# Two of five parked operands kept as sums, and the low parts of the gate and branch weights on VectorE

## The chip, the cores and the metric

The kernel runs on one core of a Trainium2 chip. The metric is the device time of one execution in microseconds, median of the runs. TensorE's granted clock in the profile has two levels, 2.4 GHz (shown as 1.00) and 1.2 GHz; a number between the two is a mean over a stretch.

## The reference

One block over 1024 latent tokens of width 1024 and 256 context tokens: a token mixer with two branches (a spatial gating unit A, a two-way gated linear recurrence B) and a convolutional feed-forward part, each with modulation from a conditioning vector. Cut to what the change touches:

```python
merged = sigmoid(gate_a) * (y_a @ w_a) + sigmoid(gate_b) * (y_b @ w_b)   # gate_a, gate_b: columns of h @ w_in
...
mod = silu(c) @ ada_w + ada_b                                            # six rows of 1024: shifts, scales, gates
...
a, v = split(h2 @ w_up)
out = (gelu(dwconv_grid(a)) * v) @ w_down                                # (1024 x 2816) @ (2816 x 1024)
```

Everything is float32.

## The kernel before

**Products in three terms.** Each float32 operand is split into a high part (a cast, on ScalarE) and a low part (operand minus high part). `mm3` issues three matmuls into the same PSUM bank: high by high (L98), high part of the weight by low part of the activations (L99), low part of the weight by high part of the activations (L100). So the third needs the weight's low part, two matmuls behind the first. `split_unit` makes both parts of a weight (L79 the cast, L80 the subtraction) and has GpSimd subtract where its caller names no other engine; `load_unit` loads a 512 KB weight tile (L86) and splits it.

**Buffers.** The loaded tiles (`wraw`), the high parts (`whi`) and the low parts (`wlo`) have three buffers each (`W_RAW, W_SPL = 3, 3`). All that follows shares them. A new tile takes the buffer whose last use is over; for a split that is being stored, when its store has landed.

**The gate stage** (966 to 1348 us of the trace). For each of 8 column blocks there is a gate of A, a branch product of A, a gate of B and a branch product of B; below they are called GA0 to GA7, A0 to A7, GB0 to GB7 and B0 to B7. Each of the 32 is one 512 KB weight tile and 48 matmuls of 512 columns. TensorE takes GA0, A0, GA1, A1 and so on to GA7, A7, then GB0, GB1, B0, GB2, B1 and so on to GB7, B6, B7. `gate` calls `project` (PSUM bank `pj`), `branch` calls `load_unit` itself (bank `hg`). After each tile comes one `mod_step`: a 512 KB block of `ada_w` is loaded into the single `maw` buffer (L841), and VectorE multiplies it by a column and adds it up (L842); every eighth step matmuls with a column of ones (L847) sum the partitions. The finished branch tile is multiplied by its gate on VectorE (L889 for A, L905 and L906 for B).

**Parked operands.** The feed-forward product at the end is done with sums of quarters of the matrices, seven products for eight. For six row units u of `w_down` (the last of them half as long) the generator `parts_down` loads four quarters (L107), makes the sums t1, t3, t2, t4 (L125, VectorE), splits them and b22 (L120 on ScalarE, L121 on VectorE), and stores both parts to DRAM (L123, on SP's queue). It runs between the tiles of the gate stage: two steps after each A tile to A5, three after each B tile. Its order is that of the source with the scheduler of the framework over it; every queue is served in order.

**The down stage.** `product_d` takes a function that gives the weight operand of a unit: `split_b` loads a quarter and splits it (L1278 on ScalarE, L1279 on VectorE), `parts_b` loads the two stored parts of a parked operand (L1268). The products run in the order X (two of them, 1897 to 1961), W with t2, Y with t1 (1991 to 2021), Z with t3 (2021 to 2051), Y with b22, Z with t4.

Of the kernel before, what the change touches and what calls it, by code (L numbers as in the profile page):

```python
# [8 lines left out]
F32 = mybir.dt.float32  # L9
# [7 lines left out]
P = 128  # L17
# [3 lines left out]
KC = D // P  # L21
# [14 lines left out]
def kernel(  # L36
# [6 lines left out]
    nc = tc.nc  # L43
# [12 lines left out]
    wp, close_wp = pool("wp", "left")  # L56
    dram, close_dram = pool("dram", space=DRAM)
# [6 lines left out]

    NU = (NJ // 2 + 1) // 2
    B_NAMES = ("b22", "t1", "t2", "t3", "t4")
    w_d = {(i, u): [dram.tile([P, 1024], F32, name=f"{i}{x}_d{u}") for x in "hl"] for i in B_NAMES for u in range(NU)}
    s2_d = [dram.tile([P, 1024], F32, name=f"s2_d{u}") for u in range(NU)]

    def unit_len(u):  # L70
        return min(2, NJ // 2 - 2 * u)

    W_RAW, W_SPL = 3, 3
    last_load = [None]
# [8 lines left out]
    def load_unit(src, k0, nk, c0, ncol, lo_eng=None):  # L83

        raw = wp.tile([P, 1024], F32, tag="wraw", name="wraw", bufs=W_RAW)
        last_load[0] = nc.sync.dma_start(  # L86
            out=raw.rearrange("p (k n) -> p k n", n=ncol),
            in_=src[k0 * P:(k0 + nk) * P, c0:c0 + ncol].rearrange("(k p) n -> p k n", p=P),
        )
        hi, lo = split_unit(raw, lo_eng)  # L90
        v = lambda t: t.rearrange("p (k n) -> p k n", n=ncol)
        return v(hi), v(lo)
# [9 lines left out]
    def raw_down(u, half, c0):  # L102

        raw = wp.tile([P, 1024], F32, tag="wraw", name="wraw", bufs=W_RAW)
        nk, r0 = unit_len(u), (half * (NJ // 2) + 2 * u) * P
        raw = raw[:, 0:nk * 512]
        last_load[0] = nc.sync.dma_start(  # L107
            out=raw.rearrange("p (k n) -> p k n", n=512),
            in_=w_down[0][r0:r0 + nk * P, c0:c0 + 512].rearrange("(k p) n -> p k n", p=P))
        return raw  # L110

    def parts_down():

        for u in range(NU):
            n = unit_len(u) * 512

            def keep(i, raw):
                hi = wp.tile([P, 1024], F32R, tag="whi", name="whi", bufs=W_SPL)[:, 0:n]
                lo = wp.tile([P, 1024], F32R, tag="wlo", name="wlo", bufs=W_SPL)[:, 0:n]
                nc.scalar.copy(out=hi, in_=raw)  # L120
                nc.vector.tensor_tensor(out=lo, in0=raw, in1=hi.bitcast(F32), op=ALU.subtract)  # L121
                for t, d_ in zip((hi, lo), w_d[i, u]):
                    nc.sync.dma_start(out=d_[:, 0:n], in_=t.bitcast(F32))  # L123

            sub = lambda o, a, b: nc.vector.tensor_tensor(out=o, in0=a, in1=b, op=ALU.subtract)  # L125
            b12, b11 = raw_down(u, 0, 512), raw_down(u, 0, 0)
            sub(b11, b12, b11)
            keep("t1", b11)
            yield
            b22 = raw_down(u, 1, 512)  # L130
            keep("b22", b22)
            yield
            sub(b12, b22, b12)
            keep("t3", b12)
            yield
            sub(b22, b22, b11)
            keep("t2", b22)
            yield
            b21 = raw_down(u, 1, 0)
            sub(b21, b21, b22)  # L140
            keep("t4", b21)
            yield
# [18 lines left out]
    for d in range(2):  # L161
        nc.gpsimd.affine_select(
            out=trif, in_=ones, pattern=[[1 if d == 0 else -1, P]], base=0,
# [21 lines left out]
    rows = {}  # L185
# [72 lines left out]
    for k in range(KC):  # L258
# [9 lines left out]
        if k == 4:  # L268
            norm_pair(ctok, ins_of(last_macc))
            ctp_ps = []  # L270
            for kk in range(KC // 2):
                tp = hg()
                ctp_ps.append(tp)
                for j in range(2):
                    for i in range(2):
                        nc.tensor.transpose(out=tp[:, (2 * j + i) * P:(2 * j + i + 1) * P],
                                            in_=ctok[:, i, (2 * kk + j) * P:(2 * kk + j + 1) * P], identity=ident)
# [63 lines left out]
    for q in range(4):  # L341
# [3 lines left out]
        for k in range(KC):  # L345
            wh, wl = units[k // 4]
# [192 lines left out]
    def project(off, h, dst_fn, lo_eng=None):  # L539

        wh, wl = load_unit(WI, 0, KC, off + h * P, P, lo_eng)
        for s in range(2):
            ps = pj()
            for k in range(KC):
                mm3(ps, (wh[:, k, :], wl[:, k, :]),
                    (hxh[k][:, s * 512:(s + 1) * 512], hxl[k][:, s * 512:(s + 1) * 512]), k == 0, k == KC - 1)
            dst_fn(s, ps)
# [42 lines left out]
    for h in range(NH):  # L590
# [46 lines left out]
        for st in range(2):  # L637
# [45 lines left out]
            for j in range(2):  # L683
                sp = hg()
                spv = sp.rearrange("p (i d t) -> p i d t", i=2, d=2)
                for i in range(2):
                    n = 2 * j + i
# [89 lines left out]
    for q in range(4):  # L777
# [4 lines left out]
        for n2 in range(NT // 2):  # L782
            ps = v_early[n2] if q == 0 and n2 < len(v_early) else token_major(units, n2)
            for j in range(2):
                n = 2 * n2 + j
                gelus.append(nc.scalar.activation(out=vt[n][:, q * 256:(q + 1) * 256],
                                                  in_=ps[:, j * 256:(j + 1) * 256], func=AF.Gelu_apprx_tanh))
# [70 lines left out]
    def gate(off, m):  # L858
        sg = gp.tile([P, T], F32, tag="sg", name="sg", bufs=2)

        def out_(s, ps):
            nc.scalar.activation(out=sg[:, s * 512:(s + 1) * 512], in_=ps, func=AF.Sigmoid)

        project(off, m, out_)
        mod_step()
        return sg

    def branch(w, m, yh, yl, fn):
        wh, wl = load_unit(w, 0, KC, m * P, P)
        for s in range(2):  # L870
            ps = hg()
            for k in range(KC):
                mm3(ps, (wh[:, k, :], wl[:, k, :]),
                    (yh[k][:, s * 512:(s + 1) * 512], yl[k][:, s * 512:(s + 1) * 512]), k == 0, k == KC - 1)
            fn(s, ps)
        mod_step()
# [117 lines left out]
    for q in range(4):  # L994
        units = [load_unit(w_o[0], 4 * u, 4, q * 256, 256, nc.vector) for u in range(2)]
        cs = slice(q * 256, (q + 1) * 256)
        for n in range(NT):
            ps = pj()
            for k in range(KC):
                wh, wl = units[k // 4]  # L1000
# [60 lines left out]
    for lo_, hi_, bias in ((0, 5 * NJ, False), (5 * NJ, 9 * NJ, True)):  # L1061
        crow = cv.tile([P, T], F32, tag="hd", name="crow", bufs=2)[:, 0:P]
        n = hi_ - lo_
# [4 lines left out]
        m = n + (NJ if bias else 0)  # L1068
# [167 lines left out]
    A11, A12, A21, A22 = quarter_a(0, 0), quarter_a(1, 0), quarter_a(0, 1), quarter_a(1, 1)  # L1236
# [25 lines left out]
    def parts_b(i):  # L1262
        def f(u):
            n = unit_len(u) * 512
            pair = []
            for x, d_ in zip(("whi", "wlo"), w_d[i, u]):
                t = wp.tile([P, 1024], F32R, tag=x, name=x, bufs=W_SPL)[:, 0:n]
                last_load[0] = nc.sync.dma_start(out=t.bitcast(F32), in_=d_[:, 0:n])  # L1268
                pair.append(v2(t, u))
            return pair  # L1270
        return f

    def split_b(half, c0):
        def f(u):
            raw, n = raw_down(u, half, c0), unit_len(u) * 512
            hi = wp.tile([P, 1024], F32R, tag="whi", name="whi", bufs=W_SPL)[:, 0:n]
            lo = wp.tile([P, 1024], F32R, tag="wlo", name="wlo", bufs=W_SPL)[:, 0:n]
            nc.scalar.copy(out=hi, in_=raw)  # L1278
            nc.vector.tensor_tensor(out=lo, in0=raw, in1=f32(hi), op=ALU.subtract)  # L1279
            return v2(hi, u), v2(lo, u)  # L1280
        return f

    def product_d(acc, fa, fb, first, tail=0, done=None, post=()):


        post = list(post)

        def mm(n, a, b, u, i):
            sl = slice(n * P, (n + 1) * P)
            k = 2 * u + i  # L1290
            mm3(acc[n], (a[0][:, i, sl], a[1][:, i, sl]), (b[0][:, i, :], b[1][:, i, :]), first and k == 0,
                k == HK - 1, skip_group_check=not first)

        late = []
        for u in range(NU):
            b = fb(u)
            a = parts_a(fa(u))
            if u > 0 and post:
                with tc.issue_after(ins_of(a_hi[-1])), tc.issue_after(ins_of(a_lo[-1])):
                    for f in post.pop(0):  # L1300
                        f()
            if u >= NU - tail:
                late.append((a, b, u))
                continue
            for i in range(unit_len(u)):
                for n in range(4):
                    mm(n, a, b, u, i)
        for n in range(4):
            for a, b, u in late:
                for i in range(unit_len(u)):  # L1310
                    mm(n, a, b, u, i)
            if done is not None:
                done(n)
# [30 lines left out]
    W, X = banks("wz"), banks("xy")  # L1344
# [54 lines left out]
    def run(*fs):  # L1399
        return [[lambda f=f, n=n: f(n) for f in fs] for n in range(4)]  # L1400
# [3 lines left out]
    def rows(n):  # L1404
        def f():
            with tc.issue_after(ins_of(last_load[0])):
                for _ in range(n):
                    next(more, None)
        return [f]

    product_d(X, A11, split_b(0, 0), True, post=[rows(3)] * 5)
    for n in range(4):
        nc.scalar.copy(out=p1[:, n, :], in_=X[n])
    product_d(X, A12, split_b(1, 0), False, post=[rows(4)] * 2)
    product_d(W, S2, parts_b("t2"), True, post=run(end_11a))
    Y, Z = banks("xy"), banks("wz")
    product_d(Y, S1, parts_b("t1"), True, post=run(end_w, end_11b))
    product_d(Z, S3, parts_b("t3"), True, post=run(end_y))
    product_d(Y, S4, parts_b("b22"), False, post=run(end_22))
    product_d(Z, A22, parts_b("t4"), False, tail=3, done=end_21,  # L1420
              post=[[lambda f=f, n=n: f(n) for f, n in g] for g in ends])
# [39 lines left out]
```

## Time and profile before

| | us |
|---|---|
| median of 3 runs | 2124.27 (2121.86 to 2124.37) |
| profiled execution, its own time | 2126.31 |
| its span | 2124.6 |
| TensorE busy | 2051.6 (97%) |
| VectorE / ScalarE / GpSimd busy | 1258.5 / 783.1 / 561.8 |
| gate stage, 966 to 1348 | 382.0 |
| Y and Z of the down stage, 1991 to 2050.7 | 59.7 |

The profiled execution lies 2.0 us over the median, and 1.7 us of it lie around the span. In the rows below a time in front is microseconds from the span's start; a bracket after a row is how long the engine was idle before it and what ended that. PE is TensorE, DVE VectorE, ACT ScalarE, POOL GpSimd, SP the queue that issues most DMAs.

### The profile page before, as it was taken

How to read it: one execution, taken by the hardware profiler on the slowest of the kernel's cores; microseconds unless marked ns; L12 is line 12 of the kernel's file. 1: busy time of each engine (PE TensorE's matmuls, PEld its weight loads, DVE VectorE, ACT ScalarE, POOL GpSimd, SP SyncE). 2: the span in 40 equal slices, each digit the busy share in tenths (PEclk: the TensorE clock that was granted, in tenths of full speed). 3: DMA queues.
4: the chain of work that ended last, by engine and by line, in shares of the span. 5: the costliest groups of instructions: out<-in, count | busy, mean ns of one | idle time of the engine just before them, and what ended most of it. 6: DMA issues, size and time to landing. Idle time of an engine off the chain costs nothing. (4 is left out here: it accounts for less than half of the span.)

```text
span 2124.6 us, 27641 instructions
## 1 busy us (share of the span) xinstructions
PE 2051.6 (97%) x11138; PEld 1736.9 (82%) x11138; DVE 1258.5 (59%) x1742; ACT 783.1 (37%) x1103; POOL 561.8 (26%) x328
## 2 busy tenths in 40 slices
PE   8889999999999999999999998999999999999997
PEld 3879889889889889888777876898778888887886
DVE  4784364374375362444343445548699888896665
ACT  3765355255355341222213222324333333334222
POOL 2131212122121110221112111134476666610001
PEclk9989999999999999999999999999999999999999
DMA  7630111111111011115564766631222222266676
GB/s 268 208 90 21 50 40 40 41 41 48 41 32 60 31 56 54 41 40 179 188 227 152 236 225 224 207 96 38 67 78 81 89 90 84 75 242 223 223 272 228
DMA packets 215138, 251.04 MB, mean 118 GB/s; under 512 B 8852, under 2 KB 166873, under 8 KB 213986
## 3 DMA queue, kind: packets, MB, share of 16 engines
q1 hardware_dynamic: 212977, 244.29, 35.0%
q10 hardware_dynamic: 2032, 4.99, 0.6%
q8 instruction: 87, 1.43, 0.3%
q14 instruction: 42, 0.34, 0.1%
HBM read 193.39 MB, written 55.85 MB: 117 GB/s over the span
## 5 line engine op out<-in xcount | busy, mean ns | idle before, releaser
L80 POOL TENSOR_TENSOR wlo<-wraw,whi 128x1024 fp32r<-128x1024 f32 x88 | 220.5, 2509 | 747.8 <-ACT whi L79 697.4
L98 PE MATMUL pj<-hxh,whi 128*128 128x512 f32 x896 | 355.7, 397 | 9.0 <-ACT whi L79 8.8
L100 PE MATMUL pj<-hxh,wlo 128*128 128x512 f32 x896 | 354.3, 395 | 8.0 <-POOL wlo L80 8.0
L99 PE MATMUL pj<-hxl,whi 128*128 128x512 f32 x896 | 353.1, 394 | 1.0 <-POOL hxl L456 1.0
L79 ACT CAST whi<-wraw 128x1024 fp32r<-128x1024 f32 x124 | 129.1, 1048 | 300.1 <-PE pj L99 131.9
L1178 DVE SCALAR_TENSOR_TENSOR acc<-apad,cw,acc 128x1024 f32<-128x1024 f32 x176 | 226.3, 1286 | 20.8 <-ACT acc L1176 17.4
L98 PEld LDWEIGHTS pj<-hxh,whi 128*128 128x128 f32 x896 | 170.2, 190 | 45.8 <-ACT whi L79 11.9
L100 PEld LDWEIGHTS pj<-hxh,wlo 128*128 128x128 f32 x896 | 169.9, 190 | 44.8 <-POOL wlo L80 10.6
L99 PEld LDWEIGHTS pj<-hxl,whi 128*128 128x128 f32 x896 | 170.0, 190 | 34.8 <-POOL hxl L456 1.3
L98 PE MATMUL pj<-whi,hxh 128*128 128x256 f32 x512 | 145.3, 285 | 0.0
L99 PE MATMUL pj<-wlo,hxh 128*128 128x256 f32 x512 | 145.1, 284 | 0.0
L100 PE MATMUL pj<-whi,hxl 128*128 128x256 f32 x512 | 144.9, 283 | 0.0
L371 DVE TENSOR_TENSOR_SCAN b<-scanm,g 128x512 f32<-128x512 bf16 (+1 forms) x24 | 26.3, 1094 | 176.7 <-ACT g L618 174.7
L842 DVE SCALAR_TENSOR_TENSOR acc<-maw,sc,acc 128x1024 f32<-128x1024 f32 x32 | 51.3, 1603 | 86.3 <-DMA maw<-in_ada_w_dram 83.2
L99 PEld LDWEIGHTS pj<-wlo,hxh 128*128 128x128 f32 x512 | 98.2, 192 | 0.4 <-issue 0.2
L98 PEld LDWEIGHTS pj<-whi,hxh 128*128 128x128 f32 x512 | 98.1, 192 | 0.4 <-issue 0.2
L100 PEld LDWEIGHTS pj<-whi,hxl 128*128 128x128 f32 x512 | 98.3, 192 | 0.0
L173 POOL TENSOR_TENSOR rs<-ss,mhalf 128x4 f32<-128x4 f32 (+1 forms) x21 | 19.6, 934 | 261.6 <-DVE ss L737 210.8
L120 ACT CAST whi<-wraw 128x1024 fp32r<-128x1024 f32 (+1 forms) x30 | 29.4, 979 | 133.4 <-DVE wraw L125 22.6
L173 POOL TENSOR_TENSOR ss<-ss,mhalf 128x1 f32<-128x1 f32 x16 | 11.2, 699 | 246.9 <-DVE ss L1333 213.4
L98 PE MATMUL pj<-whi,mh 128*128 128x256 f32 x256 | 73.6, 288 | 1.3 <-ACT mh L801 1.3
L100 PE MATMUL pj<-whi,ml 128*128 128x256 f32 x256 | 73.2, 286 | 0.8 <-DVE ml L802 0.8
(471 smaller groups left out, 5156.7 us busy)
## 6 DMA issues: line engine op xcount, KB each, us to landing
wraw<-in_w_in_dram SPq DMA_DIRECT2D x96, 512.0 KB
wraw<-in_ffn_w_up_dram SPq DMA_DIRECT2D x44, 512.0 KB
maw<-in_ada_w_dram SPq DMA_DIRECT2D x32, 512.0 KB
wraw<-in_ffn_w_down_dram SPq DMA_DIRECT2D x30, 512.0 KB
hid_d<-hd SPq DMA_DIRECT2D x22, 512.0 KB
ring<-in_ada_w_dram SPq DMA_DIRECT2D x8, 1024.0 KB
ring<-in_x_dram SPq DMA_DIRECT2D x4, 1024.0 KB
yb_d<-og SPq DMA_DIRECT2D x8, 512.0 KB
```

The lines of the kernel that those rows point to most:

```text
L79: nc.scalar.copy(out=hi, in_=raw)
L80: (lo_eng or nc.gpsimd).tensor_tensor(out=lo, in0=raw, in1=hi.bitcast(F32), op=ALU.subtract)
L98: nc.tensor.matmul(ps, lhsT=ah, rhs=bh, start=first, stop=False, **kw)
L99: nc.tensor.matmul(ps, lhsT=ah, rhs=bl, start=False, stop=False, **kw)
L100: nc.tensor.matmul(ps, lhsT=al, rhs=bh, start=False, stop=last, **kw)
L120: nc.scalar.copy(out=hi, in_=raw)
L173: nc.gpsimd.tensor_tensor(out=dst, in0=src, in1=mhalf[:, :n], op=ALU.pow)
L371: nc.vector.tensor_tensor_scan(out=b, data0=scanm[:, :n], data1=g, initial=0.0, op0=ALU.mult, op1=ALU.add)
L842: nc.vector.scalar_tensor_tensor(out=acc, in0=aw, scalar=sc[:, k, 0:1], in1=acc, op0=ALU.mult, op1=ALU.add)
L1178: nc.vector.scalar_tensor_tensor(out=grid(acc), in0=src, scalar=w_, in1=grid(acc), op0=ALU.mult, op1=ALU.add)
```

## The change

t1 and t3 are no longer split in the gate stage. Their sum is stored once, straight from the raw buffer, and the down stage loads the sum and splits it there, in the way in which it splits the operands that were never parked. The other three (b22, t2, t4) stay as they are. `gate` and `branch` name VectorE for the low part of their weights.

```diff
-    w_d = {(i, u): [dram.tile([P, 1024], F32, name=f"{i}{x}_d{u}") for x in "hl"] for i in B_NAMES for u in range(NU)}
+    w_d = {(i, u): [dram.tile([P, 1024], F32, name=f"{i}{x}_d{u}") for x in ("s" if i in ("t1", "t3") else "hl")]
+           for i in B_NAMES for u in range(NU)}
...
             def keep(i, raw):
+                if len(w_d[i, u]) == 1:
+                    nc.sync.dma_start(out=w_d[i, u][0][:, 0:n], in_=raw)
+                    return
                 hi = wp.tile([P, 1024], F32R, tag="whi", name="whi", bufs=W_SPL)[:, 0:n]
...
-        project(off, m, out_)
+        project(off, m, out_, nc.vector)
...
-        wh, wl = load_unit(w, 0, KC, m * P, P)
+        wh, wl = load_unit(w, 0, KC, m * P, P, nc.vector)
...
-    def split_b(half, c0):
+    def summed_b(i):
         def f(u):
-            raw, n = raw_down(u, half, c0), unit_len(u) * 512
+            raw = wp.tile([P, 1024], F32, tag="wraw", name="wraw", bufs=W_RAW)[:, 0:unit_len(u) * 512]
+            last_load[0] = nc.sync.dma_start(out=raw, in_=w_d[i, u][0][:, 0:unit_len(u) * 512])
+            return raw
+        return split_b(f)
...
-    product_d(Y, S1, parts_b("t1"), True, post=run(end_w, end_11b))
-    product_d(Z, S3, parts_b("t3"), True, post=run(end_y))
+    product_d(Y, S1, summed_b("t1"), True, post=run(end_w, end_11b))
+    product_d(Z, S3, summed_b("t3"), True, post=run(end_y))
```

SP's queue around GA4, before (L86 loads a gate or branch weight, L107 a quarter of `w_down`, L123 stores a part, h or l, of a parked operand; the row with t1h stands ahead of GA3's weight, the one with b22l ahead of GA4's):

```order
L123 DMA t1h_d_97<-whi 128x1024
L86 DMA wraw<-in_w_in_dram 128x8x128
L123 DMA t1l_d_98<-wlo 128x1024
L86 DMA wraw<-in_w_branch_a_dram 128x8x128
L107 DMA wraw<-in_ffn_w_down_dram 128x2x512
L123 DMA b22h_d_85<-whi 128x1024
L123 DMA b22l_d_86<-wlo 128x1024
L86 DMA wraw<-in_w_in_dram 128x8x128
L123 DMA t3h_d_121<-whi 128x1024
L123 DMA t3l_d_122<-wlo 128x1024
```

and after (t3s is the sum; the line numbers are 1 to 4 higher):

```order
L87 DMA wraw<-in_w_in_dram 128x8x128
L87 DMA wraw<-in_w_branch_a_dram 128x8x128
L108 DMA wraw<-in_ffn_w_down_dram 128x2x512
L120 DMA t3s_d_114<-wraw 128x1024
L127 DMA b22h_d_85<-whi 128x1024
L127 DMA b22l_d_86<-wlo 128x1024
L87 DMA wraw<-in_w_in_dram 128x8x128
L87 DMA wraw<-in_w_branch_a_dram 128x8x128
```

One store of t3's sum, ahead of the stores of b22 and of GA4's weight, stands for the two of its parts behind it; t1's has gone ahead of this piece.

SP's queue around GB7, before (its weight is the last row):

```order
L123 DMA t4h_d_139<-whi 128x1024
L841 DMA maw<-in_ada_w_dram 128x1024
L123 DMA t4l_d_140<-wlo 128x1024
L123 DMA t1h_d_105<-whi 128x512
L107 DMA wraw<-in_ffn_w_down_dram 128x512
L841 DMA maw<-in_ada_w_dram 128x1024
L123 DMA t1l_d_106<-wlo 128x512
L123 DMA b22h_d_93<-whi 128x512
L123 DMA b22l_d_94<-wlo 128x512
L86 DMA wraw<-in_w_in_dram 128x8x128
```

and after:

```order
L127 DMA t4h_d_127<-whi 128x1024
L845 DMA maw<-in_ada_w_dram 128x1024
L127 DMA t4l_d_128<-wlo 128x1024
L120 DMA t1s_d_100<-wraw 128x512
L108 DMA wraw<-in_ffn_w_down_dram 128x512
L845 DMA maw<-in_ada_w_dram 128x1024
L127 DMA b22h_d_93<-whi 128x512
L127 DMA b22l_d_94<-wlo 128x512
L87 DMA wraw<-in_w_in_dram 128x8x128
```

The weight keeps its place behind b22's stores; one store is gone, and t1's needs no cast.

VectorE from GB6 to GB7, before (L125 sums, L121 subtracts for a parked operand):

```order
L125 TENSOR_TENSOR wraw<-wraw 128x1024
L905 TENSOR_TENSOR sg<-hg,sg 128x512
L842 SCALAR_TENSOR_TENSOR acc<-maw,sc,acc 128x1024
L906 TENSOR_TENSOR mg_8111<-mg_8111,sg 128x512
L121 TENSOR_TENSOR wlo<-wraw,whi 128x1024
L125 TENSOR_TENSOR wraw<-wraw 128x512
L842 SCALAR_TENSOR_TENSOR acc<-maw,sc,acc 128x1024
L121 TENSOR_TENSOR wlo<-wraw,whi 128x512
```

and after (L81 is the low part of a weight: GB6's, then B5's):

```order
L81 TENSOR_TENSOR wlo<-wraw,whi 128x1024
L846 SCALAR_TENSOR_TENSOR acc<-maw,sc,acc 128x1024
L81 TENSOR_TENSOR wlo<-wraw,whi 128x1024
L909 TENSOR_TENSOR sg<-hg,sg 128x512
L129 TENSOR_TENSOR wraw<-wraw 128x1024
L910 TENSOR_TENSOR mg_8099<-mg_8099,sg 128x512
L846 SCALAR_TENSOR_TENSOR acc<-maw,sc,acc 128x1024
L125 TENSOR_TENSOR wlo<-wraw,whi 128x1024
L129 TENSOR_TENSOR wraw<-wraw 128x512
```

The low parts of the weights stand between multiply-accumulates (L842, now L846), each of which waits for its own load. TensorE's order is the same before and after; GpSimd loses 32 rows.

## Rows read from the trace of the kernel before

**Rows 1.** Busy time by window: length, each engine's busy us (instructions), clock, DMA share, GB/s.
```profile
966.00:1348.00 382.00, 365.11 (x1559) 292.99 (x1557) 175.13 (x161) 96.48 (x112) 73.26 (x30) 0.98 0.62 205
```

**Rows 2.** Waits of TensorE, 966 to 1348: line, waited for: total us, times, longest.
```profile
PE pj L98 <- ACT whi L79: 8.8, 4, 5.4
PE pj L100 <- POOL wlo L80: 8.0, 5, 1.9
```

**Rows 3.** Windows around GA4, after it, around GA6 and GB7 (columns of rows 1).
```profile
1056.80:1074.70 17.90, 14.08 (x50) 10.60 (x49) 6.88 (x8) 5.08 (x6) 4.72 (x2) 0.81 0.58 184
1074.70:1085.60 10.90, 10.90 (x50) 9.01 (x48) 2.55 (x2) 2.60 (x3) 4.79 (x2) 1.00 0.86 274
1107.10:1123.20 16.10, 13.21 (x51) 10.16 (x50) 7.21 (x4) 3.08 (x4) 4.74 (x2) 0.89 0.41 134
1303.90:1324.40 20.50, 13.90 (x51) 10.50 (x50) 10.32 (x8) 3.73 (x5) 4.75 (x2) 0.83 0.48 148
```

**Rows 4.** Timeline at GA4: start, duration, engine, line, operation, idle time before it.
```profile
1051.39 0.61 SPq L123 DMA_DIRECT2D t3h_d<-whi  x1
...
1058.15 1.04 ACT L79 CAST whi<-wraw 128x1024 fp32r<-128x1024 f32 x1 [6.29 <-DMA t3h_d<-whi]
...
1059.24 0.50 PE L98 MATMUL pj<-hxh,whi 128*128 128x512 f32 x1 [1.87 <-ACT whi L79]
...
1062.00 0.79 PE L100 MATMUL pj<-hxh,wlo 128*128 128x512 f32 x1 [1.95 <-POOL wlo L80]
```

**Rows 5.** Timeline at GB7 (columns of rows 4).
```profile
1296.44 0.43 SPq L107 DMA_DIRECT2D wraw<-in_ffn_w_down_dram  x1
...
1300.87 0.62 ACT L120 CAST whi<-wraw 128x512 fp32r<-128x512 f32 x1 [4.33 <-DMA wraw<-in_ffn_w_down_dram]
...
1302.97 0.38 SPq L86 DMA_DIRECT2D wraw<-in_w_in_dram  x1
...
1308.59 1.04 ACT L79 CAST whi<-wraw 128x1024 fp32r<-128x1024 f32 x1 [6.60 <-DMA wraw<-in_w_in_dram]
...
1309.68 0.80 PE L98 MATMUL pj<-hxh,whi 128*128 128x512 f32 x1 [5.39 <-ACT whi L79]
```

**Rows 6.** Groups by line, 966 to 1348: busy us, mean ns, idle us before and releasers.
```profile
L80 POOL TENSOR_TENSOR wlo<-wraw,whi 128x1024 fp32r<-128x1024 f32 x30 | 73.3, 2442 | 305.6 <-ACT whi L79 257.4 <-DMA t3l_d<-wlo 16.9 <-DMA t2l_d<-wlo 15.9
L842 DVE SCALAR_TENSOR_TENSOR acc<-maw,sc,acc 128x1024 f32<-128x1024 f32 x32 | 51.3, 1603 | 86.3 <-DMA maw<-in_ada_w_dram 83.2 <-DMA acc<-in_ada_b_dram 3.1
...
L121 DVE TENSOR_TENSOR wlo<-wraw,whi 128x1024 fp32r<-128x1024 f32 (+1 forms) x30 | 35.9, 1195 | 29.4 <-ACT whi L120 14.6 <-DMA t3l_d<-wlo 4.2 <-DMA t2l_d<-wlo 3.5
```

**Rows 7.** Durations min/median/max in ns, waits for the load, and two timeline rows.
```profile
L842 DVE SCALAR_TENSOR_TENSOR acc<-maw,sc,acc x32: 1271/1285/3397, 977.9 to 1309.9; 128x1024 f32<-128x1024 f32 x32
...
  DMA maw<-in_ada_w_dram: 83.2, 26
...
L80 DVE TENSOR_TENSOR wlo<-wraw,whi x2: 1212/1214/1216, 1342.4 to 1344.2; 128x1024 fp32r<-128x1024 f32 x2
...
1108.79 3.38 DVE L842 SCALAR_TENSOR_TENSOR acc<-maw,sc,acc 128x1024 f32<-128x1024 f32 x1 [6.21 <-DMA maw<-in_ada_w_dram]
...
1108.74 2.35 POOL L80 TENSOR_TENSOR wlo<-wraw,whi 128x1024 fp32r<-128x1024 f32 x1 [23.80 <-ACT whi L79]
```

**Rows 8.** Down stage: windows of Y and Z; groups by line, 1913 to 2060.
```profile
1991.00:2020.80 29.80, 29.80 (x133) 24.66 (x132) 17.97 (x21) 7.96 (x12) 0.00 (x0) 1.00 0.55 192
2020.80:2050.70 29.90, 29.90 (x134) 24.75 (x133) 14.43 (x16) 5.89 (x6) 0.00 (x0) 1.00 0.75 261
...
L99 PE MATMUL xy<-wlo,b21h 128*128 128x512 f32 x79 | 31.4, 398 | 1.2 <-DVE wlo L1279 1.2
L98 PE MATMUL xy<-whi,b21h 128*128 128x512 f32 x78 | 31.2, 400 | 1.1 <-ACT whi L1278 1.1
...
L1279 DVE TENSOR_TENSOR wlo<-wraw,whi 128x1024 fp32r<-128x1024 f32 (+1 forms) x9 | 9.9, 1103 | 4.7 <-ACT whi L1278 4.6
L1278 ACT CAST whi<-wraw 128x1024 fp32r<-128x1024 f32 (+1 forms) x9 | 8.6, 953 | 5.9 <-DMA wraw<-in_ffn_w_down_dram 3.5 <-PE xy L100 2.4
```

More of the change, by code (lines that the diff above doesn't have):

```diff
@@ L1271, in parts_b, with plain_b, split_b, f @@
         return f
-    def split_b(half, c0):
+    def summed_b(i):
         def f(u):
-            raw, n = raw_down(u, half, c0), unit_len(u) * 512
+            raw = wp.tile([P, 1024], F32, tag="wraw", name="wraw", bufs=W_RAW)[:, 0:unit_len(u) * 512]
+            last_load[0] = nc.sync.dma_start(out=raw, in_=w_d[i, u][0][:, 0:unit_len(u) * 512])
+            return raw
+        return split_b(f)
+    def plain_b(half, c0):
+        return split_b(lambda u: raw_down(u, half, c0))
+    def split_b(load):
+        def f(u):
+            raw, n = load(u), unit_len(u) * 512
             hi = wp.tile([P, 1024], F32R, tag="whi", name="whi", bufs=W_SPL)[:, 0:n]
@@ L1409, in rows @@
         return [f]
-    product_d(X, A11, split_b(0, 0), True, post=[rows(3)] * 5)
+    product_d(X, A11, plain_b(0, 0), True, post=[rows(3)] * 5)
     for n in range(4):
         nc.scalar.copy(out=p1[:, n, :], in_=X[n])
-    product_d(X, A12, split_b(1, 0), False, post=[rows(4)] * 2)
+    product_d(X, A12, plain_b(1, 0), False, post=[rows(4)] * 2)
     product_d(W, S2, parts_b("t2"), True, post=run(end_11a))
     Y, Z = banks("xy"), banks("wz")
-    product_d(Y, S1, parts_b("t1"), True, post=run(end_w, end_11b))
-    product_d(Z, S3, parts_b("t3"), True, post=run(end_y))
+    product_d(Y, S1, summed_b("t1"), True, post=run(end_w, end_11b))
+    product_d(Z, S3, summed_b("t3"), True, post=run(end_y))
     product_d(Y, S4, parts_b("b22"), False, post=run(end_22))
```

## The prediction, made before the changed kernel ran

> **What bounds the kernel now.** I read the page's busy shares and the TensorE line first: TensorE is busy for nearly the whole span, so only its waits and the stretches at a lower granted clock can be saved. I then cut the trace by stage. The change touches the gate stage, 966 to 1348 us, and two products of the down stage, 1991 to 2051 us. In the gate stage [rows 1] TensorE works 32 weight tiles of 48 matmuls; a tile takes 10.9 us where nothing waits, as the last window of [rows 3] shows (1074.7 to 1085.6, clock 1.00). 32 × 10.9 = 349 us, some 5 us go to the small matmuls with the ones column, and the stage takes 382. The view of TensorE's waits names what is over [rows 2]: 8.8 us for the high part of an input-projection weight (ScalarE, line 79) and 8.0 us for the low part (GpSimd, line 80), nine waits and 16.8 us in all. The windows around the three worst [rows 3] show what such a wait costs beside itself: granted clock 0.81, 0.89 and 0.83 instead of 1.00, so 17.9 × 0.19 + 16.1 × 0.11 + 20.5 × 0.17 = 8.7 us at the 1.2 GHz level, always behind a wait. Together **25.5 us** can be had in this stage, no more. In the down stage from 1917 to 2098 the view of waits holds no TensorE row, so nothing can be had there.
>
> **Why it waits.** Two mechanisms. The first is the low part itself: the third matmul of a group wants it 0.46 us after the first, and GpSimd needs 2.44 us on average [rows 6]. At gate weight GA4 (1059.24) TensorE starts with the high part, then stops 1.95 us for the low one [rows 4]. The second is the parked splits: gate and branch weights share three high and three low buffers with the splits that are being stored. At GA4 the high buffer was held by the store of t3's high part, issued at 1051.39; the cast ended its wait for it at 1058.15, 6.8 us later [rows 4]. Near the stage's end (GB7) the weight's load is the last of a series on SP's queue: b22's at 1296.44, the weight itself only at 1302.97; cast at 1308.59, and TensorE stood 5.39 us [rows 5].
>
> **Low parts on VectorE.** 32 subtractions leave GpSimd and take 1.214 us each on VectorE, as the two that stand there now show [rows 7]. Each low part ends 2.44 − 1.21 = 1.2 us earlier behind its cast, if VectorE is free. The five low-part waits shrink from 8.0 to 8.0 − 5 × 1.2 = 2.0 us at most, with no other edit. VectorE pays 32 × 1.21 = 38.8 us; twelve parked subtractions of line 121 leave (12 × 1.195 = 14.3), and its multiply-accumulates of line 842 shorten: median 1.285, mean 1.603 [rows 6, 7]; the long ones lie beside GpSimd (1108.79, 3.38 us long, beside 1108.74, 2.35 long). With GpSimd silent, 32 × 0.32 = 10.2 us come back. Net +14 us on 175 of 382 [rows 1]: an average of half busy, so the place in the queue decides, not the sum. The price of that is the second rival.
>
> **Two operands stored as sums.** t1 and t3 leave out a cast, a subtraction and one store per unit (six units each, the last half as long), and take no high or low buffer; in exchange the raw buffer stays taken until the one store lands. At GA4 the hop "b22's store lands, cast of t3, t3's store lands" (6.8 us and more) goes, and the weight's buffer is behind b22's store instead. A multiply-by-gate of a finished branch tile (line 889) now stands behind such low parts too; the bank it frees is wanted a whole tile later, so 0. I worked the new orders of SP, VectorE and ScalarE forward by hand, with 4.5 to 5 us for a 512 KB transfer, between the 4.4 us of b22's half-sized load (1296.44 to 1300.87) and the 5.6 to 6.8 us of the weight's load at GB7 and t3's store at GA4 [rows 4, 5]. GA3 has its high part near 1024, wanted at 1031.7. Its split frees the next raw buffer that much earlier, b22 lands near 1037.5, sum 1.2, t3's store to 1043.5, GA4's load to 1048, cast 1049, low part 1050.3; it is wanted at 1055.1 (all earlier waits gone). GA5 and GA6 come out 8 to 9 us early. So in the first half everything goes: about 8.2 us of waits and 5.2 of clock, **−13.4**. In the second half GB3, GB4 and GB5 come out 5 to 8 us early. GB6 is closer: low part 0.7 us ahead of need. GB7: counted from GB6's start (1280.3), t1's load is issued about 4 us earlier than now (low part of GB6 and of the branch weight 1.2 us sooner each, and no wait at GB6), b22 no longer waits behind t1's split, and the weight's load is issued at +15 instead of +22.5; the high part is there at +20.5 to +21.6, the low at +21.8 to +22.9, wanted at +21.8. That is on the edge: a hop of the chain that takes 1 us more makes TensorE wait, and the clock may fall once (1.8 to 3.5 us, by [rows 3]). I put 3 us of waits and 1.5 of clock back, between 0 and 8: second half 12.1 − 4.5, **−7.6**.
>
> The Trainium skill (SBUF — State Buffer, section "The DMA setup-cost knee (why "@ 1 MiB" ≠ asymptote)") gives a transfer as 2 us plus its bytes over 436 GB/s, which makes an estimate of 3.2 us for 512 KB. The transfers of [rows 4, 5] took 5.6 and 6.8, so the trace does not agree here, where several are under way at once. By the page GB6 and GB7 would be early and the sum −25.5; by the rows it is −21.
>
> **The down stage.** In products Y and Z one raw load replaces two part loads; twelve casts (0.95 us) and twelve subtractions (1.10 us) come in [rows 8]. Per product that is 6 × 1.10 = 6.6 us on VectorE (busy 18.0 and 14.4 of 29.8) and 5.7 us on ScalarE (8.0 and 5.9): cover is there. The raw buffers are otherwise unused in these products, so the loads can go ahead of those they replace. The nearest row for what the split costs TensorE is the first product of this stage, which splits in the same way: 1.2 us of waits for a low part (and 1.1 for a high one) in twelve units, at its start [rows 8]. Below nothing is excluded, since TensorE does not wait in Y and Z now. I take **0**, up to +2.3 for one late start. Transfers of 5.8 MB each way go; no engine waits for their sum, so 0.
>
> **Sum.** −13.4 − 7.6 + 0 = −21.0 on the profiled run: 2126.3 − 21.0 = 2105.3; that run is 2.0 us over the median, so I forecast **2104.5** (by the bounds 2099 to 2112).
>
> **Rivals.** (a) *Transfers are fast enough at GB6 and GB7*: nothing comes back, −25.5, **2100**. The lighter DMA load speaks for it, the lengths in [rows 4, 5] against. This is what the page's rule gives. Chance 0.13. (b) *The parked part buys nothing*: the raw buffers, now held until a store lands, make the weights' loads late by what the split buffers cost now, and the high-part waits stay. Then only the low parts gain: 8.0 − 2.0 = 6, **2118 to 2120**, or **2122** if the clock falls once more. For it: store (to 6.8 us), load (5.6), cast and subtraction lie in one chain at GA4, 15 us and more. Against: 22 us (two tiles) are there. Chance 0.13. (c) *VectorE's queue takes the wait over*, and the kernel is slower. The low part now stands behind a multiply-accumulate that waits for its load: line 842 made VectorE idle 83.2 us before 26 of 32 [rows 6, 7], 3.2 us each, and takes 1.3 itself. A low part caught there comes 4.5 us late, and each such tile costs that, since GpSimd, which waited for nobody, had 2.4. From seven full catches (31 us) on the gain is gone and more; at eight it is 36 − 25.5 = +10.5, **2135**. For it: in VectorE's new order 14 of the low parts have such a row one or two places ahead. Against: apart from GB6 and GB7 the low parts have 5 us and more to spare, and the loads run ahead of them. Chance 0.12. The Trainium skill (PSUM — Partial Sum Buffer, section "Engine vs sequencer instructions") says that VectorE's queue is strictly first in, first out; the 83.2 us of idleness before line 842, with finished casts behind it, agree.
>
> **How the numbers follow.** Forecast 0.60, (a) 0.13, (b) 0.13, (c) 0.12, others 0.02. A measurement of this kernel tells 0.2% (4.2 us) from no change: faster is below 2120, slower above 2128.5. Faster: 0.60 + 0.13 + 0.03 of (b) and 0.01 = 0.77; same: 0.10 of (b) and 0.01 = 0.11; slower 0.12. The range goes from 2097 (case (a) and the run's scatter) to 2121 (most of (b)); (c) and the rest of (b) lie outside.
>
> **What would show it.** Right: the gate stage near 361 us; TensorE's waits there 1 to 5 us in all and only at GB6 and GB7; clock 1.00 around GA4 and GA6; GpSimd busy about 73 us less [rows 1, 6]; line 842 near 1.29 us; no TensorE wait in Y and Z. Wrong: high-part waits at GA3, GA4 or GA6 again, behind the landing of a sum's store (b); low-part waits whose VectorE row follows an idle line 842 (c); or a stage that does not shorten although the waits are gone.

## The result, and the profile after

The changed kernel takes **2100.47 us** (median of 4 runs, 2095.67 to 2101.46) beside 2124.32 of the kernel before: a ratio of 0.988 (95% interval 0.9856 to 0.9904), 25 us. Run again later beside other runs of before it took 2097.69 (ratio 0.9876, 0.9856 to 0.9897). The profiled execution took 2101.34, its span is 2099.6, 25.0 us less than before.

The stages, from the start and end of TensorE's matmuls in the timelines of the two profiled executions (the gate stage ends here at 1347.5 and 1326.1, where the last of the small matmuls with the ones column behind B7 starts):

| us | before | after | difference | forecast |
|---|---|---|---|---|
| start of GA0 | 966.5 | 968.4 | +1.8 | 0 |
| GA0 to GB0 (first half of the gate stage) | 191.2 | 178.2 | −13.1 | −13.4 |
| GB0 to the end of the stage (second half) | 189.8 | 179.6 | −10.2 | −7.6 |
| end of the stage to the first up projection of the feed-forward part | 157.4 | 153.4 | −4.0 | 0 |
| up projection | 391.8 | 390.5 | −1.3 | 0 |
| the two X products | 64.3 | 65.1 | +0.8 | 0 |
| W, Y, Z and Y again, each | 29.92 | 29.92 | 0 | 0 |
| last product | 33.4 | 34.4 | +1.0 | 0 |

I read the rows of +1.8, −1.3, +0.8 and +1.0 as scatter: over the ten runs below GA0 starts between 964.3 and 969.4, and the up projection takes 388.2 to 391.6, in no order of what was changed.

The view of busy time by window, the gate stage alone before and after (length, then TensorE, its weight loads, VectorE, ScalarE, GpSimd with instruction counts, clock, DMA share, GB/s):

```profile
966.50:1347.50 381.00, 364.11 (x1554) 292.49 (x1553) 174.13 (x161) 95.62 (x111) 73.26 (x30) 0.98 0.62 205
```

```profile
968.30:1326.10 357.80, 356.47 (x1554) 288.90 (x1553) 183.01 (x183) 85.90 (x99) 0.00 (x0) 1.00 0.61 200
```

GpSimd is empty, VectorE has 9 us more, the clock is 1.00. The view of TensorE's waits in the same stretch of after, which answers [rows 2]:

```profile
PE pj L99 <- ACT whi L80: 0.8, 1, 0.8
PE pj L101 <- DVE wlo L81: 0.5, 1, 0.5
```

Of 16.8 us in nine waits 1.3 in two are left, both at GB7, and in the second profile of the same kernel there is none. The timeline there (start, duration, what it waited for), beside [rows 5]:

```profile
1278.00 0.87 SPq L108 DMA_DIRECT2D wraw<-in_ffn_w_down_dram  x1
...
1284.73 0.38 SPq L87 DMA_DIRECT2D wraw<-in_w_in_dram  x1
...
1290.05 1.04 ACT L80 CAST whi<-wraw 128x1024 fp32r<-128x1024 f32 x1 [6.79 <-DMA wraw<-in_w_in_dram]
...
1291.15 0.50 PE L99 MATMUL pj<-hxh,whi 128*128 128x512 f32 x1 [0.80 <-ACT whi L80]
1291.48 0.40 PE L100 MATMUL pj<-hxl,whi 128*128 128x512 f32 x1
1292.41 0.50 PE L101 MATMUL pj<-hxh,wlo 128*128 128x512 f32 x1 [0.53 <-DVE wlo L81]
```

The weight's load is issued 5.6 us before TensorE is done with the tile in front (1291.15 − 0.80 = 1290.35); before it was 1.3 us (1309.68 − 5.39 = 1304.29, and 1302.97). The groups by line, answering [rows 6] and [rows 7]:

```profile
L846 DVE SCALAR_TENSOR_TENSOR acc<-maw,sc,acc 128x1024 f32<-128x1024 f32 x32 | 41.1, 1284 | 45.2 <-DMA maw<-in_ada_w_dram 45.1
L81 DVE TENSOR_TENSOR wlo<-wraw,whi 128x1024 fp32r<-128x1024 f32 x32 | 39.0, 1221 | 60.2 <-ACT whi L80 50.5 <-DMA t4l_d<-wlo 4.5 <-DMA b22l_d<-wlo 3.4
```

```profile
L846 DVE SCALAR_TENSOR_TENSOR acc<-maw,sc,acc x32: 1277/1284/1289, 981.8 to 1292.3; 128x1024 f32<-128x1024 f32 x32
```

The multiply-accumulates are all 1.28 us long (before: 1.271 to 3.397), and the time for which they make VectorE wait for their load fell from 83.2 to 45.1 us. The windows of Y and Z, answering [rows 8]:

```profile
1965.00:1994.80 29.80, 29.80 (x133) 24.68 (x132) 23.89 (x27) 13.18 (x18) 0.00 (x0) 1.00 0.29 97
1994.90:2024.70 29.80, 29.80 (x133) 24.66 (x133) 19.38 (x21) 9.37 (x10) 0.00 (x0) 1.00 0.43 147
```

VectorE has 5 to 6 us more in each, TensorE is without a gap as before.

### The profile page after: what moved, and what is told of

Its sections match the earlier page's. It is cut to its first block, busy times and chain, and to the rows that moved or that the text cites. A ratio compares the mean times of both kernels' runs of the same rounds, so it can differ in the third digit from the quotient of the medians.

```text
span 2099.6 us, 27515 instructions
## 1 busy us (share of the span) xinstructions
PE 2044.8 (97%) x11138; PEld 1734.7 (83%) x11138; DVE 1275.0 (61%) x1774; ACT 782.9 (37%) x1103; POOL 482.9 (23%) x296
## 5 line engine op out<-in xcount | busy, mean ns | idle before, releaser
L81 POOL TENSOR_TENSOR wlo<-wraw,whi 128x1024 fp32r<-128x1024 f32 x56 | 142.6, 2551 | 421.2 <-ACT whi L80 419.0
L81 DVE TENSOR_TENSOR wlo<-wraw,whi 128x1024 fp32r<-128x1024 f32 x68 | 82.6, 1220 | 114.5 <-ACT whi L80 104.8
L1015 POOL TENSOR_TENSOR xa<-tg,a2b 128x256 f32<-128x256 f32 x32 | 29.7, 929 | 450.2 <-DMA a2b<-mod_d 404.3
L100 PE MATMUL pj<-wlo,mh 128*128 128x256 f32 x256 | 72.4, 283 | 0.0
```

What stands on the lines that cost most here:

```text
L81: (lo_eng or nc.gpsimd).tensor_tensor(out=lo, in0=raw, in1=hi.bitcast(F32), op=ALU.subtract)
L100: nc.tensor.matmul(ps, lhsT=ah, rhs=bl, start=False, stop=False, **kw)
L1015: nc.gpsimd.tensor_mul(out=xa[n][:, cs], in0=tg, in1=a2b[:, cs])
```

## The experiments

Gains below are worked out from the ratios, as a share of 2124.3 us; their intervals are 3 to 7 us to either side.

**Each half of the change alone.** The theory on trial was that of the prediction: the parked splits hold the buffers, so the sums carry most of the gain (some 15 to 20 us), and the move to VectorE carries about 6. The rival: the engine alone.

The sums alone, low parts on GpSimd:

```diff
-        project(off, m, out_, nc.vector)
+        project(off, m, out_)
...
-        wh, wl = load_unit(w, 0, KC, m * P, P, nc.vector)
+        wh, wl = load_unit(w, 0, KC, m * P, P)
```

> t1 and t3 are stored as sums, the low parts of the gate and branch weights stay on GpSimd. My theory (the store of a parked split in front of a weight's buffer is the cause, the 2.4 us of GpSimd only makes it worse): in the changed kernel the weights up to GB5 had their parts 5 us or more ahead, so 1.2 us more each does no harm there, and the waits at GA3, GA4, GA6 stay away; every hop of the chain to GB6 and GB7 is 1.2 us longer, so 3 to 7 us of waits come there. Gate stage 361 to 368 us instead of 358, time 2104 to 2112. Rival (GpSimd's low part binds whatever comes before): about 8 us of low-part waits as before, with their clock, time 2112 to 2118. VectorE's line for the multiply-accumulate stays at a mean of 1.5 us or more by both.

Measured: 2110.11 (ratio 0.9931, 0.9914 to 0.9949). The first half of the gate stage is without a wait (178.1 us), the second has not gained at all: 191.2 us, 189.8 before. The windows and the waits:

```profile
969.40:1147.50 178.10, 178.10 (x779) 144.51 (x777) 66.51 (x59) 36.85 (x43) 39.82 (x17) 1.00 0.57 185
1147.50:1338.80 191.30, 182.89 (x777) 147.06 (x776) 99.01 (x95) 48.67 (x57) 34.14 (x14) 0.97 0.62 203
```

```profile
PE pj L99 <- ACT whi L80: 5.0, 2, 3.3
PE pj L101 <- POOL wlo L81: 3.4, 2, 1.7
```

The time lies in the theory's range and the place of the waits is right (GB6 and GB7); the waits are 8.4 us instead of 3 to 7, and the stage takes 369.4 us instead of 361 to 368.

The low parts alone, all five operands in parts (the edit is the reverse of the one above, on the kernel before):

> The low parts of the gate and branch weights go to VectorE, all five parked operands keep their two stored parts. My theory: the high-part waits stay (7 to 9 us, GA4 and GB7 above all), the low-part ones shrink from 8.0 to 1 to 3 us, and the clock falls as often: time 2115 to 2120. Rival (engines alone: 1.2 us less on each hop that frees a raw buffer and an undisturbed VectorE pull the whole chain forward): waits of 2 to 4 us in all, time 2103 to 2108. A third possibility is that the longer VectorE queue makes it 2124 or more.

Measured: **2097.03** (0.9867, 0.9847 to 0.9888). The theory had 2115 to 2120; the rival's 2103 to 2108 was still too slow. The gate stage is at its floor, 355.9 us, and the view of TensorE's waits holds no row in it:

```profile
967.50:1323.40 355.90, 355.90 (x1555) 289.00 (x1553) 196.11 (x195) 96.76 (x111) 0.00 (x0) 1.00 0.67 222
```

So the move to VectorE does everything that the whole change does, and the high-part waits go with it although every parked split is still there. The theory fell. The rival was right in kind (shorter hops pull the whole chain forward), and too small in size.

One sum at a time, low parts on VectorE: first t3, then t1 (the same edit the other way round).

```diff
-    w_d = {(i, u): [dram.tile([P, 1024], F32, name=f"{i}{x}_d{u}") for x in ("s" if i in ("t1", "t3") else "hl")]
+    w_d = {(i, u): [dram.tile([P, 1024], F32, name=f"{i}{x}_d{u}") for x in ("s" if i in ("t3",) else "hl")]
...
-    product_d(Y, S1, summed_b("t1"), True, post=run(end_w, end_11b))
+    product_d(Y, S1, parts_b("t1"), True, post=run(end_w, end_11b))
```

> As the changed kernel, but only t3 is a sum; t1 keeps its two parts. Theory: t3's split stood ahead of GA4 and GA6, t1's ahead of GA3 and GB7; so GA4 and GA6 stay clean, GB7 waits 3 to 5 us for its high part with one fall of the clock: 2104 to 2110. Rival (every parked split is alike, half of them gives half): 2110 to 2113.

> As the changed kernel, but only t1 is a sum; t3 keeps its two parts. Theory: the waits at GA4 and GA6 come back for the high part (2 to 4 us in all, one or two falls of the clock), GB7 stays within 2 us: 2105 to 2112. Rival (half gives half): 2110 to 2113.

Measured: 2097.20 (0.9874, 0.9848 to 0.9900) with t3 alone, 2096.95 (0.9868, 0.9844 to 0.9892) with t1 alone. Both expectations missed in the same way: the waits hardly came back where a part was parked again. With t3 alone GB7 waits 1.7 us instead of 3 to 5 (1.3 in the first profile of the changed kernel), with t1 alone nothing waits.

**What the engine does: its duration, or its silence.** Why should a high part come earlier because low parts are made elsewhere? The timelines show what follows a low part. Before, GA3 and A3:

```profile
1031.53 2.36 POOL L80 TENSOR_TENSOR wlo<-wraw,whi 128x1024 fp32r<-128x1024 f32 x1 [18.31 <-ACT whi L79]
1040.28 2.39 POOL L80 TENSOR_TENSOR wlo<-wraw,whi 128x1024 fp32r<-128x1024 f32 x1 [6.39 <-ACT whi L79]
```

```profile
1033.91 0.38 SPq L86 DMA_DIRECT2D wraw<-in_w_branch_a_dram  x1
1042.69 0.38 SPq L107 DMA_DIRECT2D wraw<-in_ffn_w_down_dram  x1
1047.60 0.34 SPq L123 DMA_DIRECT2D b22h_d<-whi  x1
```

GA3's low part ends at 1033.89, and A3's load is issued at 1033.91. A3's low part ends at 1042.67, and b22's load is issued at 1042.69; then come b22's split, its store, t3's split, its store ([rows 4]) and GA4. The low part is the last reader of the raw buffer, so it lies in one chain with what is loaded after it. It is so not only here: from 966.5 to 1347.5 the view of the waits of SP's queue (line, waited for: total us, times, longest) has 14 weight loads and 13 loads of quarters that waited for a low part on GpSimd, 27 of the 56 loads into raw buffers that the trace has there:

```profile
SPq L86 <- POOL wlo L80: 51.1, 14, 5.3
SPq L107 <- POOL wlo L80: 37.9, 13, 5.0
```

The same stretch with only the low parts moved:

```profile
1026.26 1.23 DVE L80 TENSOR_TENSOR wlo<-wraw,whi 128x1024 fp32r<-128x1024 f32 x1 [3.34 <-DMA t1l_d<-wlo]
...
1032.10 1.23 DVE L80 TENSOR_TENSOR wlo<-wraw,whi 128x1024 fp32r<-128x1024 f32 x1 [2.32 <-ACT whi L79]
```

```profile
1027.52 0.38 SPq L86 DMA_DIRECT2D wraw<-in_w_branch_a_dram  x1
1033.36 0.38 SPq L107 DMA_DIRECT2D wraw<-in_ffn_w_down_dram  x1
1038.19 0.34 SPq L123 DMA_DIRECT2D b22h_d<-whi  x1
```

Here, too, each load is issued 0.03 us behind the end of a low part; from one load to the next it is 5.84 us (before 8.78), and b22's store has come forward by 9.4 us. Of these 2.9 us the shorter low part is 1.2; most of the rest is A3's load, which takes 3.5 us up to its cast instead of 5.2, and why it does no run shows. The casts of A3's high part, before and with the low parts moved, and below them the cast for GA4:

```profile
1039.14 1.05 ACT L79 CAST whi<-wraw 128x1024 fp32r<-128x1024 f32 x1 [7.25 <-DMA wraw<-in_w_branch_a_dram]
```

```profile
1031.02 1.05 ACT L79 CAST whi<-wraw 128x1024 fp32r<-128x1024 f32 x1 [4.43 <-DMA wraw<-in_w_branch_a_dram]
...
1047.30 1.05 ACT L79 CAST whi<-wraw 128x1024 fp32r<-128x1024 f32 x1 [4.86 <-DMA t3h_d<-whi]
```

GA4's cast still waits for the store of t3's high part, as in [rows 4]; but TensorE comes to GA4 only at 1056.58, 9 us later. Three experiments tell apart what in that counts. The first does the subtraction twice on VectorE:

```diff
         (lo_eng or nc.gpsimd).tensor_tensor(out=lo, in0=raw, in1=hi.bitcast(F32), op=ALU.subtract)
+        if twice:
+            lo_eng.tensor_tensor(out=lo, in0=raw, in1=hi.bitcast(F32), op=ALU.subtract)
...
-        project(off, m, out_, nc.vector)
+        project(off, m, out_, nc.vector, True)
...
-        wh, wl = load_unit(w, 0, KC, m * P, P, nc.vector)
+        wh, wl = load_unit(w, 0, KC, m * P, P, nc.vector, True)
```

> The kernel with only the low parts moved to VectorE (no waits in the gate stage, 2097), with each of these 32 subtractions done twice there in a row, so that a low part takes 2.44 us as it did on GpSimd; GpSimd stays silent. Theory A (duration: the low part frees the raw buffer, and so every load, sum and store behind it, and 1.2 us on each of these hops was what the chain lacked): the waits come back, 8 to 20 us in all, time 2108 to 2126. Theory B (GpSimd itself: it made VectorE's instructions longer, 10 us of them, and the order of the queues was another): the waits stay under 4 us, time 2096 to 2103.

Measured: 2116.59 (0.9957, 0.9943 to 0.9971): 9 us gained instead of 28, as theory A has it. The gate stage takes 377.8 us, 21.9 more than with one subtraction and 3.2 less than before; GpSimd is silent, the multiply-accumulates are undisturbed, and the waits are back, high-part ones first:

```profile
PE pj L100 <- ACT whi L79: 10.9, 2, 8.0
PE pj L102 <- DVE wlo L82: 5.2, 3, 2.9
```

```profile
L844 DVE SCALAR_TENSOR_TENSOR acc<-maw,sc,acc 128x1024 f32<-128x1024 f32 x32 | 41.0, 1281 | 30.4 <-DMA maw<-in_ada_w_dram 30.3
```

They lie at GA6, GB6 and GB7; GA3 and GA4 are clean. The second subtraction also keeps VectorE busy longer (229.7 of 377.8 us, 34 us more than with one); this experiment doesn't tell how much of the 21.9 us is that. Nor does it tell what the 9 us that stay gained come from: 3.2 of them lie in the stage and 4.0 behind it.

The other two move the low parts of one half of the weights, with all operands in parts: the gates', then the branches'.

```diff
-        project(off, m, out_)
+        project(off, m, out_, nc.vector)
```

> All five operands parked in parts, low parts on VectorE for the 16 gate weights alone; the 16 branch weights stay on GpSimd. Local theory (the low part matters where the third matmul waits for it, and all such waits were at gates): nearly all of the gain, 2097 to 2103. Chain theory (each low part frees a raw buffer): half of the slack is missing, 2 to 8 us of waits come back, high-part ones first, 2102 to 2112.

```diff
-        wh, wl = load_unit(w, 0, KC, m * P, P)
+        wh, wl = load_unit(w, 0, KC, m * P, P, nc.vector)
```

> The other half: low parts on VectorE for the 16 branch weights alone, gates on GpSimd. Local theory: nothing is gained, since no wait was at a branch weight, 2121 to 2127. Chain theory: a gain of 6 to 15 us although no branch weight ever waited, 2109 to 2118, with the low-part waits at the gates shorter or gone.

Measured: gates alone 2115.11 (0.9950, 0.9933 to 0.9968), branches alone **2109.94** (0.9926, 0.9906 to 0.9947). The waits, gates moved, then branches moved:

```profile
PE pj L98 <- ACT whi L79: 8.4, 5, 4.0
PE pj L100 <- DVE wlo L80: 2.1, 4, 0.5
```

```profile
PE pj L98 <- ACT whi L79: 5.7, 1, 5.7
PE pj L100 <- POOL wlo L80: 4.4, 3, 2.4
```

With the gates moved the low-part waits shrink to what the prediction said, 2.1 us, and the high-part ones stay at 8.4. The gain is 10.6 us: in the profile the stage is 7.8 us shorter (373.2 us), and behind it the 4.0 us are gone as in the changed kernel. Both expectations missed: 2115.1 is slower than either range, and 10.5 us of waits are left where the chain theory had 2 to 8. With the branches moved, where TensorE had not waited once, 15.7 us are gained, as the chain theory had it (2109 to 2118); the low-part waits at the gates, still on GpSimd, fall from 8.0 to 4.4 and the high-part ones from 8.8 to 5.7. Their loads start earlier: counted from GA0's start, GA4's is issued at 78.0 us instead of 84.3, and at 73.8 with all low parts moved. With the gates alone moved it is issued at 84.2: up to GA4 the low parts of the gates brought nothing forward by themselves. So the branch half bears the chain theory out; what a gate's low part adds to the chain was not taken apart. The two halves make 26 us together, the whole move 28; with these intervals that doesn't tell whether they simply add.

**What the sums are worth.** The changed kernel again, beside the runs of the last three:

> The changed kernel again, beside the same runs of the kernel before as the three others, for its distance to the kernel with only the low parts moved (2097.0). If the two sums cost something: 2099 to 2102, with the wait at GB7 again; if they are indifferent: 2096 to 2099.

Measured: 2097.69 (0.9876, 0.9856 to 0.9897), with no wait at GB7 this time. Beside 2097.03 without the sums they are indifferent. Then the sums carried on, first to all operands (t2 and t4 as sums too, b22 not parked; the diff shows this one), then only b22 taken out, with t2 and t4 in parts:

```diff
-    w_d = {(i, u): [dram.tile([P, 1024], F32, name=f"{i}{x}_d{u}") for x in ("s" if i in ("t1", "t3") else "hl")]
+    w_d = {(i, u): [dram.tile([P, 1024], F32, name=f"{i}{x}_d{u}") for x in ("s" if i != "b22" else "hl")]
...
-            keep("b22", b22)
...
-    product_d(W, S2, parts_b("t2"), True, post=run(end_11a))
+    product_d(W, S2, summed_b("t2"), True, post=run(end_11a))
...
-    product_d(Y, S4, parts_b("b22"), False, post=run(end_22))
-    product_d(Z, A22, parts_b("t4"), False, tail=3, done=end_21,
+    product_d(Y, S4, plain_b(1, 512), False, post=run(end_22))
+    product_d(Z, A22, summed_b("t4"), False, tail=3, done=end_21,
```

> The changed kernel taken to its end: t1, t2, t3 and t4 are all stored as sums, b22 is not parked at all (the down stage loads it from w_down), so no parked operand is split in the gate stage; every product of the down stage splits its own. Low parts on VectorE. Theory (with the low parts on VectorE the chain has slack and the sums neither help nor harm; the down stage has cover for the splits): gate stage at its floor of 356 us, Y, Z and W at 29.9, the wait of the last product for t4's part (2.4 us) smaller: 2094 to 2099. Rival (each sum holds a raw buffer until its store lands, and three per unit make the weights late): 3 to 10 us of high-part waits in the second half, 2100 to 2110.

> The changed kernel, with b22 not parked (the down stage loads it from w_down and splits it); t2 and t4 stay in parts. Two stores per unit less and no raw buffer held longer. Theory: 2095 to 2099, the same as the changed kernel within its scatter, with no wait at GB7. Rival (the split in the product after Z is not covered, since VectorE is busier there): 1 to 4 us of waits in that product, 2099 to 2103.

Measured: 2095.57 (0.9857, 0.9833 to 0.9881) and 2096.58 (0.9862, 0.9831 to 0.9893), both where the theory had them. With no split parked at all the gate stage stands at the floor that it had with all five parked, although VectorE has 162.4 us of work there instead of 196.1 and the DMA queues move 167 GB/s instead of 222:

```profile
964.30:1320.10 355.80, 355.80 (x1554) 289.00 (x1553) 162.38 (x164) 68.53 (x83) 0.00 (x0) 1.00 0.53 167
```

W, Y, Z and the second Y take 29.92 us in it as in all kernels here, with all seven products splitting their weights; the last one takes 31.9 us, and 33.3 in the kernel with the low parts alone. It is the fastest of all that ran, by 1.5 us on the kernel with the low parts alone, which the runs don't tell from nothing.

## Why the prediction was right, and where it was not

The time (2104.5 forecast, 2100.5 measured, range 2097 to 2121) and the sign were right. The reading of the gate stage was right too: 25.5 us were to be had, and the stage is 25.1 us shorter in the kernels that reach its floor. What the time came from was not, and that the total came out all the same is in part luck: both edits draw on the same 25 us, the forecast spent 21 of them, and the edit that it priced as the smaller one, the low parts, takes them all by itself. The sum also slips at its end: 2105.3 less the 2.0 us by which the profiled run lies over the median is 2103.3 and not 2104.5. And its 8.7 us "at the 1.2 GHz level" are what the lower clock cost; at a level of half the speed the time spent there is twice that.

- **The step that failed** is "The five low-part waits shrink from 8.0 to 8.0 − 5 × 1.2 = 2.0 us at most, with no other edit", and with it the price of rival (b), 2118 to 2122. It counted a low part only where TensorE waits for it. The waits it counted did shrink to 2.1 us (gates alone); but a low part is also the last reader of a raw buffer, and 27 loads of the stage waited for one. Measured: 28 us for the low parts alone instead of 6. The prediction had used this very effect in working both edits forward together (GA3's split "frees the next raw buffer that much earlier", and GB6's low part brings GB7's loads forward), and left it out where it priced the low parts alone. So the words of rival (b), that the parked part buys nothing, came true behind the low parts, and its price was 21 us off.
- **The sums** were left with −21 us less those 6. Alone they do bring 15 (2110.1), but all in the first half and after the stage's end; behind the low parts they bring nothing that can be measured (2097.7 with them, 2097.0 without). The hand-worked forward run of the changed orders was right that GA3 and GA4 would be in time and GB7 on the edge. Counted from GA0 and GB6, GA3's high part came within 1 us of it, GA4's low part some 5 us earlier, and GB7's load 1.3 us later. It was silent on which edit made that, since it had both. It named the holding of buffers at GA4 as the cause; that hop is real ([rows 4]), but it stopped nobody once the chain ahead of it was shorter.
- **GB6 and GB7**: 3 us of waits and 1.5 of clock were put back, between 0 and 8. Over the floor of 355.9 us the stage took 1.9 us in one profile of the changed kernel (the wait at GB7 is 1.3 of it) and 0.4 in the other, with no fall of the clock: the low end of the bounds. Rival (a), 2100, came out nearest, though not for its reason: the weight's load at GB7 still took 5.3 us (1284.73 to 1290.0); it was issued earlier. There the trace goes on disagreeing with the estimate of 3.2 us worked out from the Trainium skill (SBUF — State Buffer, "The DMA setup-cost knee (why "@ 1 MiB" ≠ asymptote)"); A3's load above came near it, with 3.5.
- **Rival (c)**, VectorE's queue, did not come. In the changed kernel the only low-part wait on VectorE was 0.5 us; the multiply-accumulates wait less for their loads than before (45.1 us instead of 83.2). VectorE's +14 us was +9.
- **Down stage, 0**: right, 29.92 us for Y and for Z, to the hundredth.
- **Missed**: 4.0 us behind the gate stage. Before, the high part of B7's weight waited for t4's store to 1330.94, and the next stage's first six casts queued behind it on ScalarE. Their subtractions (L802) start on VectorE at 1333.45, and the multiplications by the gates of B6 and B7 (L905, L906) stand in its queue behind and among them: B7's last one ends at 1350.96, 4.7 us behind B7's last matmul (1346.31). The eighth cast of the next stage needs it, so TensorE waited 2.1 us, and the clock fell (0.90 from 1347.5 to 1364.9, which costs 1.7 us). After, they are in time. The rows of ScalarE, VectorE and of TensorE's waits, before:

```profile
1330.94 1.05 ACT L79 CAST whi<-wraw 128x1024 fp32r<-128x1024 f32 x1 [3.36 <-DMA t4h_d<-whi]
...
1332.38 5.79 ACT L801 CAST mh<-mg 128x1024 fp32r<-128x1024 f32 x6
...
1351.00 1.04 ACT L801 CAST mh<-mg 128x1024 fp32r<-128x1024 f32 x1 [3.00 <-DVE mg L906]
```

```profile
1333.45 4.44 DVE L802 TENSOR_TENSOR ml<-mg,mh 128x1024 fp32r<-128x1024 f32 x3 [5.15 <-ACT mh L801]
...
1350.27 0.69 DVE L906 TENSOR_TENSOR mg<-mg,sg 128x512 f32<-128x512 f32 x1
```

```profile
PE pj L98 <- ACT mh L801: 1.3, 1, 1.3
PE pj L100 <- DVE ml L802: 0.8, 1, 0.8
```

and after, where the view of waits has no row behind the stage (end 1326.1):

```profile
1301.96 1.05 ACT L80 CAST whi<-wraw 128x1024 fp32r<-128x1024 f32 x1 [2.38 <-DMA t4h_d<-whi]
...
1307.03 5.79 ACT L805 CAST mh<-mg 128x1024 fp32r<-128x1024 f32 x6
...
1326.38 1.05 ACT L805 CAST mh<-mg 128x1024 fp32r<-128x1024 f32 x1 [0.59 <-DVE mg L910]
```

The six casts start 19.1 us ahead of the stage's end instead of 15.1, and the eighth 0.3 us behind it instead of 3.5. These 4.0 us are gone in all ten runs of the experiments. With them the profiled execution is 25.0 us shorter, where the forecast had 21.0; the gate stage adds 2.3 to the forecast, and the scatter in the other rows takes 2.3 back.

What stays open: why the sums alone gain nothing in the second half. The waits there are at GB6 and GB7 as before. For GB7 the rows of that kernel tell where the gain went (SP's queue and the cast of b22; beside them [rows 5]):

```profile
1283.53 1.01 SPq L108 DMA_DIRECT2D wraw<-in_ffn_w_down_dram  x1
...
1293.62 0.33 SPq L845 DMA_DIRECT2D maw<-in_ada_w_dram  x1
1294.05 0.39 SPq L87 DMA_DIRECT2D wraw<-in_w_in_dram  x1
```

```profile
1289.79 0.62 ACT L124 CAST whi<-wraw 128x512 fp32r<-128x512 f32 x1 [3.12 <-DMA wraw<-in_ffn_w_down_dram]
```

From the end of GB6's low part (1273.70; before 1282.62) it is 9.8 us to the load of b22 instead of 13.8, and from there 10.5 to the load of GB7's weight instead of 6.5: b22's load takes 6.3 us up to its cast instead of 4.4, and the weight then stands behind a load into the single `maw` buffer, which the last multiply-accumulate frees only at 1293.59. The 4 us that the sum saves are lost again. Why b22's load took longer, and why GB6 is still late, was not taken apart.

## What to carry to other kernels

Price a step not only where somebody waits for its result, but also by what it frees: an operation that is the last reader of a buffer can lie in the chain of every load behind it, and its move, 1.2 us less on each of 32, made 28 us here although the engine itself was idle for four fifths of the stage. The view of the queue's waits names such an operation before any change is made. Where a change has two edits, work each one's arrival times through alone before giving either a share; the sum can be right and the shares wrong. A parked operand that looks like the cause because a wait ends with its store may only be the last hop of a chain that is long elsewhere.

## What the hardware showed beside that

VectorE's multiply-accumulate grew while GpSimd subtracted beside it: it took 1.603 us on average, up to 3.397, with GpSimd at work in the stage, and in the changed kernel, where GpSimd is silent there, 1.277 to 1.289 for all 32. That is 10 us of VectorE's time; since the doubled subtraction gave back most of the gain with GpSimd silent, it is not what most of the 28 us came from.
